# Transposing three of four residual chunks by DMA instead of TensorE at the stage borders of a two-layer hybrid trunk

## The chip, the cores and the metric

The kernel runs on one core of a Trainium2 chip, as one program. The metric is the device time of one execution in microseconds (us). The core's engines run side by side, each through its own list of instructions in order: PE (TensorE, matmuls and transposes), ACT (ScalarE), DVE (VectorE), POOL (GpSimd) and SP (SyncE, which here does nothing but issue DMAs). They wait for one another by semaphores.

## What is computed

Two layers over 256 tokens of width 2048. Cut to what matters here:

```
for l in range(DEPTH):                                  # 2
    hn = rms_norm(h, norm_w[l])
    proj = hn @ w_in[l]                                 # stage "in"
    y = concatenate([deltanet(proj), hgrn2(proj)])      # the two groups of heads
    h = h + y @ w_out[l]                                # stage "out"
    gate = sigmoid(h @ w_ple_gate[l])                   # stage "gate"
    h = h + (p[l] @ w_ple_up[l]) * gate                 # "up", inside the stage "gate"
return rms_norm(h, final_norm_w)
```

All is float32. The residual `h` lies with tokens on the partitions, in four tiles `h[c]` of 128 x 2 x 512 (token, half of the tokens `m`, column), one for each chunk `c` of 512 columns. A matmul needs its left operand with the contracted columns on the partitions, so each time the residual is the input of a stage it has to be transposed. This occurs at three **borders**: out to gate in layer 0 (names `g0`), gate to in of layer 1 (`n1`) and out to gate in layer 1 (`g1`).

## The kernel before

**Products.** Each weight tile is read from memory once, by a DMA of SP into one of three buffers `raw` (L415). ACT rounds it into `whi` (L434) and DVE takes the rest `wlo = raw - whi` (L436), three buffers each; the activations are taken apart in the same way into `hi` and `lo` by `split` (L507). `products` (L448) then issues three matmuls for one product: hi by hi, lo by hi, hi by lo, all at L373. A **step** is one weight tile of 128 x 1024: two slices of 128 rows, two halves of the tokens, three products, 12 matmuls of 128x512. In a step that neither starts nor ends an accumulation the eight matmuls with `whi` come first, and the four with `wlo` last.

**Order.** `run_step` (L469) writes a step's matmuls in program order, after `ahead` (L439) has asked for the preparation of weights two steps on and for loads up to four steps on, as far as the buffers go. PE's list stays in the order written; a scheduler places the instructions of ACT, DVE and SP between one another. All other work is written as generators, which `tick` (L395) moves on by one at each step: `yield 4` means four steps later. The numbers in `DELAY` and `DELAY_AT` say how many.

**Stages.** In the stages out and gate, chunks 0 and 1 of the columns alternate, then chunk 2 runs, then chunk 3. When chunk `c` of out is summed, `after_out` (L1196) adds it into `h[c]` on DVE, waits a few steps, and calls `turn`; `after_gate` (L1202) does the same behind the gate's exp and ln on ACT.

**The transposition.** `turn` (L526) moves one chunk: two banks of PSUM, each filled by four PE transposes of 128x128 (L531), and `split` reads them on ACT and DVE. So a turn costs PE eight instructions, ACT two or four, DVE as many.

**Other names.** Tag `et` has two buffers of 128 x 1024, used in the stage in by `evict` (L619). `tmp` has six of 128 x 512.

Of the kernel before, what the change touches and what calls it, by code (L numbers as in the profile page):

```python
# [8 lines left out]
F32 = mybir.dt.float32  # L9
F32R = mybir.dt.float32r  # L10
I32 = mybir.dt.int32
AF = mybir.ActivationFunctionType
ALU = mybir.AluOpType
PSUM = bass.MemoryType.PSUM
# [18 lines left out]
def chunk_cols(chunk):  # L33

    return [(START[k], 16) if k == "ba" else (START[k] + 256 * g, 256) for k, g in chunk]
# [25 lines left out]
}  # L61


def delay(kind, g, step):
    return DELAY_AT.get(f"{kind}{g}{step}", DELAY[kind][step])
# [106 lines left out]
def trunk(ctx: ExitStack, tc: tile.TileContext, head, xT, x, pT, W, par, fw, cst, msk, eye, out):  # L172
    nc = tc.nc
# [12 lines left out]
    V, S, G = nc.vector, nc.scalar, nc.gpsimd  # L186
# [3 lines left out]
    h = [hp.tile([128, 2, 512], F32, name=f"h{c}") for c in range(4)]  # L190
    pr = cp.tile([128, NPAR], F32, name="pr")
    cs = cp.tile([128, 544], F32, name="cs")
    ms = cp.tile([128, NMASK], I32, name="ms")

# [9 lines left out]
    def xk(k, n=1):  # L204
        o = (0 if k // 4 else NNW) + T * (k % 4)
        return xt[k // 4][:, o:o + T * n]
# [58 lines left out]
    def first_prep():  # L265
# [5 lines left out]
        for k, cs_ in ((0, (0, 1)), (1, (0, 1)), (2, (0,)), (3, (0,)), (2, (1,)), (3, (1,))):  # L271
            if 0 in cs_:
                kp, sl, x, sc = k // 2, slice(T * (k % 2), T * (k % 2) + T), xk(k), xt[0][:, k:k + 1]
                S.activation(a[kp][0][:, sl], x, AF.Copy, scale=sc)
            for c in cs_:
                n, wsl = unit(c, k)
                if k or c:
                    S.activation(w[n][0][:, wsl], raw[n][:, wsl], AF.Copy)
                else:
# [53 lines left out]
    def P(name, i, n=1):  # L333
        o = PAR[name][0] + i
        return pr[:, o:o + n]
# [11 lines left out]
    def gate_constants():  # L347

        S.activation(negA, P("alog", 0, DEPTH * 16), AF.Exp)
        V.tensor_scalar(negA, negA, -1.0, None, ALU.mult)  # L350
# [4 lines left out]
        for l in range(DEPTH):  # L355
            V.tensor_tensor(ee[:, l], lg[l], mx, ALU.subtract)
        S.activation(ee, ee, AF.Exp)
        den = sp.tile([128, 8], F32, tag="lb2", name="den")
# [62 lines left out]
    def prep(n):  # L421
# [11 lines left out]
        for sl in parts:  # L433
            S.activation(hi[:, sl], raw[:, sl], AF.Copy)  # L434
        for sl in parts:
# [48 lines left out]
    def tmp(name, shape=(128, 512)):  # L484
        return tp.tile([128, 512], F32, tag="tmp", name=name)

    def sigmoid(dst, src, e=None):

        if e is None:
            S.activation(dst, src, AF.Exp, scale=-1.0)  # L490
            V.tensor_scalar(dst, dst, BIG, 1.0, ALU.min, ALU.add)
# [15 lines left out]
    def split(src, kp, scales, name):  # L507

        hi = ap_.tile([128, 2 * T], F32R, tag="ahi", name=f"{name}hi{kp}")
        lo = ap_.tile([128, 2 * T], F32R, tag="alo", name=f"{name}lo{kp}")  # L510
        if scales is None:
            S.activation(hi, src, AF.Copy)
            V.tensor_tensor(lo, src, hi.bitcast(F32), ALU.subtract)
            return hi, lo
        w = 2 * T // len(scales)
        for j, sc in enumerate(scales):
            S.activation(hi[:, w * j:w * j + w], src[:, w * j:w * j + w], AF.Copy, scale=sc)
        for j, sc in enumerate(scales):
            sl = slice(w * j, w * j + w)
            V.scalar_tensor_tensor(lo[:, sl], src[:, sl], sc, hi[:, sl].bitcast(F32), ALU.mult, ALU.subtract)  # L520
        return hi, lo

    def norm_scales(l, kp):
        return [P("nw", l * KT + 2 * kp + j) for j in range(2)]

    def turn(c, name, scales):  # L526

        out = []
        for half in range(2):
            ps = pm.tile([128, 512], F32, tag="m", name=f"{name}t{c}{half}")  # L530
            for j in range(2):  # L531
                for m in range(2):
                    k = 2 * half + j
                    PE.transpose(ps[:, 256 * j + 128 * m:256 * j + 128 * m + 128], h[c][:, m, 128 * k:128 * k + 128], ident)
            out.append(split(ps, 2 * c + half, scales(2 * c + half), name))
        return out

    first_ss = []
# [51 lines left out]
    def mix(tag, n, bufs, name):  # L590
        return mp.tile([128, n], F32, tag=tag, name=name, bufs=bufs)
# [604 lines left out]
    def after_out(c, ps, hact, l):  # L1196
        for m in range(2):
            V.tensor_tensor(h[c][:, m], ps[m], h[c][:, m], ALU.add)
        yield delay("b", c, "o")
        hact[2 * c:2 * c + 2] = turn(c, f"g{l}", lambda kp: None)  # L1200

    def after_gate(c, ps, up, act, st, l):  # L1202
        t = [tmp(f"pg{l}{c}{m}") for m in range(2)]
        if l + 1 == DEPTH:
            for m in range(2):
                S.activation(t[m], ps[m], AF.Tanh, scale=0.5)
        else:
            for m in range(2):
                S.activation(t[m], ps[m], AF.Exp, scale=-1.0)
            for m in range(2):  # L1210
                V.tensor_scalar(t[m], t[m], BIG, 1.0, ALU.min, ALU.add)
            for m in range(2):
                S.activation(t[m], t[m], AF.Ln)
                S.activation(t[m], t[m], AF.Exp, scale=-1.0)
        for m in range(2):
            if l + 1 == DEPTH:
                V.scalar_tensor_tensor(t[m], t[m], 1.0, up[m], ALU.add, ALU.mult)
            else:
                V.tensor_tensor(t[m], up[m], t[m], ALU.mult)
            V.tensor_tensor(h[c][:, m], h[c][:, m], t[m], ALU.add)  # L1220
            st.add(c, m)
            if l + 1 == DEPTH:
                G.tensor_tensor(h[c][:, m], h[c][:, m], fwt[c // 2][:, 512 * (c % 2):512 * (c % 2) + 512], ALU.mult)
        if l + 1 < DEPTH:
            yield delay("b", c, "g")
            act[2 * c:2 * c + 2] = turn(c, f"n{l + 1}", lambda kp: norm_scales(l + 1, kp))

    class Finish:

# [66 lines left out]
    act = [None] * (KT // 2)  # L1296
    first_loads()
    for l in range(DEPTH):
# [25 lines left out]
        for c, k4 in order:  # L1324
# [5 lines left out]
            w = 2 if sum(n for _, n in chunk_cols(ch)) > 272 else 4  # L1330
# [30 lines left out]
        hact = [None] * (KT // 2)  # L1361
        chunks, order = stage_plan("out", l)
        ps = {}
        for c, k4 in order:
            if c not in ps:
                ps[c] = banks(f"out{l}{c}", c)
            for q in (0, 2):
                while not pairs_ready(y, k4[q:q + 2]):
                    tick()
                run_step(ps[c], y)  # L1370
            if k4[3] == OUT_KTS[-1]:
                spawn(after_out(c, ps[c], hact, l))
            if c == 2 and k4[0] == OUT_KTS[0]:
                pin = tmp(f"pin{l}")
                nc.scalar.dma_start(out=pin.rearrange("p (j t) -> p j t", j=2), in_=pT[l])
                pact = [split(pin, 0, [0.5] if l + 1 == DEPTH else None, f"p{l}")]
# [6 lines left out]
        act = [None] * (KT // 2)  # L1383
        chunks, order = stage_plan("gate", l)
        ps = {}
        for c, k4 in order:
            if c not in ps:
                ps[c] = banks(f"gate{l}{c}", c)
                if l + 1 == DEPTH and c == 3:

                    ps[c][1] = [ps[c][1], pm.tile([128, 512], F32, tag="m", name="gaterun")]
            for q in (0, 2):
                end = l + 1 == DEPTH and c == 3
                if k4[q + 1] == KT - (9 if end else 1):
                    up = [pm.tile([128, 512], F32, tag="m", name=f"up{l}{c}{m}") for m in range(2)]
                    run_step(up, pact)
                if end and k4[q + 1] == KT - 9:
                    break
                while not pairs_ready(hact, k4[q:q + 2]):
                    tick()  # L1400
                run_step(ps[c], hact)
            if end and k4[3] == KT - 9:

                n = state["next"]
                for i in range(5):
                    ahead(n + i)
                    products(n + i, 0, ps[c], hact)
                half0 = Finish(0, ps[c], up, st)
                for r in range(2):
                    for i in range(5):  # L1410
                        products(n + i, 1, ps[c], hact, run=r)
                last_norm(half0, Finish(1, ps[c], up, st))
                break
            if k4[3] == KT - 1:
                spawn(after_gate(c, ps[c], up, act, st, l))
# [35 lines left out]
```

## Time and profile before

| what | value |
|---|---|
| median of 3 runs | 1242.79 us (1240.89 to 1245.74) |
| the profiled execution: its own time | 1241.43 us |
| its span, first to last instruction | 1239.7 us |
| DVE busy over the span | 882.2 us (71%) |
| ACT busy over the span | 771.9 us (62%) |
| POOL busy over the span | 75.3 us (6%) |
| memory traffic, mean | 176 GB/s |
| border g0: out ends, gate starts | 516.85 us |
| border g1: out ends, gate starts | about 1131.6 us |

A profile lists each instruction with engine, line, tile names (`out<-in`, the buffer numbers left out) and shape. The share of busy time is a mean over stages with different limits; the **chain of work that ended last** tells what set the end, and the **waits** tell for whom an engine stood still. PE's matmuls overlap: a matmul of 128x512 lasts 0.39 us by its record, but a step of twelve takes 2.72 us, 0.227 us each. Idle time of an engine that isn't the bottleneck costs nothing.

### The profile page before, as it was taken

The numbers are of one execution on the slowest core, as the hardware profiler recorded it, in microseconds if no ns is written. First come the engines' busy times: TensorE is split into PE (matmuls) and PEld (weight loads), VectorE is DVE, ScalarE is ACT, GpSimd is POOL, SyncE is SP. The second block draws the span as 40 slices with busy tenths as digits, with TensorE's granted clock in tenths as the row PEclk, the third lists the DMA queues.
The fourth block names the chain that finished last, engine by engine and source line by source line (L and its number), as shares of the span: only waits on it lengthen the run. The fifth ranks groups of instructions, "written<-read, shape, count | busy, mean of one in ns | idle before, by whom it ended". The sixth has DMA issues, their size and how long they took to land.

```text
span 1239.7 us, 21567 instructions
## 1 busy us (share of the span) xinstructions
PE 1226.5 (99%) x8354; PEld 1030.9 (83%) x8354; DVE 882.2 (71%) x1537; ACT 771.9 (62%) x1340; POOL 75.3 (6%) x67
## 2 busy tenths in 40 slices
PE   9999999999999999999999999999999999999997
PEld 8888888888888888888888888878888888888886
DVE  7777897887568656547668878886875696555565
ACT  7676766686757644437666667674867676444453
POOL 0310000000000100000003100000000010000021
PEclk9999999999999999999999999999999999999999
DMA  8455455535354445555555555555444555655563
GB/s 289 175 193 178 158 176 179 175 136 186 140 216 153 171 178 187 180 194 188 178 183 178 178 174 175 171 178 160 133 151 142 183 155 175 207 182 179 183 204 136
DMA packets 74006, 218.69 MB, mean 176 GB/s; under 512 B 15536, under 2 KB 21040, under 8 KB 73904
## 3 DMA queue, kind: packets, MB, share of 16 engines
q1 hardware_dynamic: 63680, 211.93, 51.2%
q10 hardware_dynamic: 10224, 5.39, 1.6%
q8 instruction: 65, 1.06, 0.3%
q14 instruction: 37, 0.30, 0.1%
HBM read 212.84 MB, written 4.46 MB: 175 GB/s over the span
## 4 chain that ended last, share of the span: by engine, by line
PE 89%; DVE 5%; ACT 2%; DMA 2%; issue 1%; SPq 0%; POOLq 0%; POOL 0%; ACTq 0%; DVEq 0%
PE out L373 14%; PE gate L373 13%; PE in1dk L373 7%; PE in0dv L373 6%; PE in1dv L373 6%; PE in0hi L373 6%; PE in1hf L373 5%; PE in0dk L373 5%; PE in0hf L373 5%; PE in1hi L373 5%; DVE wlo L436 2%; PE up L373 2%; DMA raw<-W 2%; PE in0dz L373 1%; PE in1dz L373 1%
## 5 line engine op out<-in xcount | busy, mean ns | idle before, releaser
L436 DVE TENSOR_TENSOR wlo<-raw,whi 128x1024 fp32r<-128x1024 f32 (+2 forms) x393 | 479.9, 1224 | 285.1 <-ACT whi L434 280.2
L434 ACT ACTIVATE whi<-raw 128x1024 fp32r<-128x1024 f32 (+2 forms) x393 | 409.8, 1045 | 309.6 <-PE out L373 89.1
L373 PE MATMUL in1hf<-whi,n1hi 128*128 128x512 f32 x128 | 41.3, 404 | 0.0
L373 PE MATMUL in1hi<-whi,n1hi 128*128 128x512 f32 x128 | 41.0, 402 | 0.0
L373 PE MATMUL in1dk<-whi,n1hi 128*128 128x512 f32 x128 | 40.4, 397 | 0.0
L373 PE MATMUL in1hf<-whi,n1lo 128*128 128x512 f32 x128 | 40.0, 394 | 0.0
L373 PE MATMUL in1hi<-whi,n1lo 128*128 128x512 f32 x128 | 39.7, 391 | 0.0
L373 PE MATMUL gate<-whi,g0hi 128*128 128x512 f32 x128 | 39.7, 391 | 0.0
L373 PE MATMUL in1dk<-whi,n1lo 128*128 128x512 f32 x128 | 39.6, 390 | 0.0
L373 PE MATMUL gate<-whi,g0lo 128*128 128x512 f32 x128 | 39.5, 390 | 0.0
L373 PE MATMUL in1dv<-whi,n1hi 128*128 128x512 f32 (+1 forms) x128 | 36.5, 376 | 0.0
L373 PE MATMUL gate<-whi,g1hi 128*128 128x512 f32 (+1 forms) x120 | 35.7, 379 | 0.0
L373 PE MATMUL gate<-whi,g1lo 128*128 128x512 f32 (+1 forms) x120 | 35.7, 379 | 0.0
L373 PE MATMUL in1dk<-wlo,n1hi 128*128 128x512 f32 x128 | 35.6, 390 | 0.0
L373 PE MATMUL in1hf<-wlo,n1hi 128*128 128x512 f32 x128 | 35.6, 390 | 0.0
L373 PE MATMUL in1hi<-wlo,n1hi 128*128 128x512 f32 x128 | 35.6, 390 | 0.0
L373 PE MATMUL gate<-wlo,g0hi 128*128 128x512 f32 x128 | 35.6, 390 | 0.0
L373 PE MATMUL in1dv<-whi,n1lo 128*128 128x512 f32 (+1 forms) x128 | 34.9, 364 | 0.0
L373 PE MATMUL gate<-wlo,g1hi 128*128 128x512 f32 (+1 forms) x120 | 32.6, 380 | 0.0
L373 PE MATMUL in1dv<-wlo,n1hi 128*128 128x512 f32 (+1 forms) x128 | 31.5, 363 | 0.0
L373 PE MATMUL in0hi<-whi,n0hi 128*128 128x512 f32 x96 | 30.8, 402 | 0.0
L373 PE MATMUL in0hf<-whi,n0hi 128*128 128x512 f32 x96 | 30.7, 401 | 0.0
(1485 smaller groups left out, 2895.3 us busy)
## 6 DMA issues: line engine op xcount, KB each, us to landing
raw<-W SPq DMA_DIRECT2D x383, 512.0 KB, 3.6
raw<-W SPq DMA_DIRECT2D x7, 544.0 KB, 3.7
h<-x SPq DMA_DIRECT2D x4, 512.0 KB, 4.8
xt<-xT SPq DMA_DIRECT2D x3, 512.0 KB, 6.2
out_dram<-h SPq DMA_DIRECT2D x5, 256.0 KB, 2.3
di0d<-di0Bt ACTq DMA_DIRECT2D x4, 256.0 KB, 2.3
di1d<-di1Bt ACTq DMA_DIRECT2D x4, 256.0 KB, 2.3
fw<-fw ACTq DMA_DIRECT2D x2, 512.0 KB, 6.3
```

What stands on the lines that cost most here:

```text
L373: return tc.keep_in_program_order(nc.tensor.matmul(*a, **k))
L434: S.activation(hi[:, sl], raw[:, sl], AF.Copy)
L436: V.tensor_tensor(lo[:, sl], raw[:, sl], hi[:, sl].bitcast(F32), ALU.subtract)
```

## The change

For chunks 0, 1 and 2 a new `turn_by_dma` takes the place of `turn`, at all three borders; chunk 3 keeps `turn`. The DMA moves elements of 16 bits, so each float is cut into its two halves:

1. ACT copies `h[c][:, m]`, seen as 16-bit integers, into the tile `flat` (names `g0p`, `n1p`, `g1p`) with all low halves in one block and all high halves in another. One copy of 1024 elements for each `m`.
2. SP issues one transposing DMA of 128 x 2048 halves (512 KB), in 16 blocks of 128x128, into `across` (`g0q`, `n1q`, `g1q`).
3. ACT joins low and high halves again into float tiles (`g0t`, `n1t`, `g1t`), one copy of 1024 elements for each half chunk.
4. `split` goes on as before, but from these tiles and no longer from PSUM.

Both `flat` and `across` are of tag `et`, which has two buffers: one chunk takes both. `XB` holds the ticks between these parts.

```
+U16 = mybir.dt.uint16
...
+XB = 1, 1, 4, 1, 1
...
+    def turn_by_dma(c, name, scales):
+
+        u16 = lambda ap: ap.bitcast(U16)
+        flat, across = (u16(mix("et", 1024, 2, f"{name}{x}{c}")).rearrange("p (w k m b) -> p w k m b", w=2, k=4, m=2)
+                        for x in "pq")
+        for m in range(2):
+            S.copy(flat[:, :, :, m], u16(h[c][:, m]).rearrange("p (k b w) -> p w k b", k=4, w=2))
+            yield XB[m]
+        every = lambda ap: ap.rearrange("p w k m b -> p (w k m) b")
+        nc.sync.dma_start_transpose(every(across), flat.rearrange("p w k m b -> p (w k m b)"))
+        yield XB[2]
+        out = []
+        for half in range(2):
+            t = tmp(f"{name}t{c}{half}")
+            S.copy(u16(t).rearrange("p (b w) -> p w b", w=2),
+                   across[:, :, 2 * half:2 * half + 2].rearrange("p w k m b -> p w (k m b)"))
+            yield XB[3 + half]
+            out.append(split(t, 2 * c + half, scales(2 * c + half), name))
+        return out
...
     def after_out(c, ps, hact, l):
         for m in range(2):
             V.tensor_tensor(h[c][:, m], ps[m], h[c][:, m], ALU.add)
-        yield delay("b", c, "o")
-        hact[2 * c:2 * c + 2] = turn(c, f"g{l}", lambda kp: None)
+        if c < 3:
+            hact[2 * c:2 * c + 2] = yield from turn_by_dma(c, f"g{l}", lambda kp: None)
+        else:
+            yield delay("b", c, "o")
+            hact[2 * c:2 * c + 2] = turn(c, f"g{l}", lambda kp: None)
...
-            yield delay("b", c, "g")
-            act[2 * c:2 * c + 2] = turn(c, f"n{l + 1}", lambda kp: norm_scales(l + 1, kp))
+            scales = lambda kp: norm_scales(l + 1, kp)
+            if c < 3:
+                act[2 * c:2 * c + 2] = yield from turn_by_dma(c, f"n{l + 1}", scales)
+            else:
+                yield delay("b", c, "g")
+                act[2 * c:2 * c + 2] = turn(c, f"n{l + 1}", scales)
```

How it moves instructions is shown at border g0. PE's list loses 72 transposes (nine turns of eight) and is otherwise the same. First ACT's list around chunk 0; before the change (`h_85` is chunk 0 of the residual, `h_86` chunk 1; numbers of `whi` and `raw` differ between the two programs, the rows stand for the same weights):

```order
L434 ACTIVATE whi_5153<-raw_5115 128x1024 [waits DMAHW7_49,DVE_49,PE_49]
L434 ACTIVATE whi_5173<-raw_5133 128x1024 [waits DMAHW0_49,DVE_49,PE_49]
L434 ACTIVATE whi_5191<-raw_5151 128x1024 [waits DMAHW1_49,DVE_49,PE_49]
L434 ACTIVATE whi_5213<-raw_5171 128x1024 [waits DMAHW2_49,DVE_49,PE_49]
L434 ACTIVATE whi_5249<-raw_5189 128x1024 [waits DMAHW3_49,DVE_49,PE_49]
```

And with the change:

```order
L548 COPY g0p_5171<-h_85 128x8x128 [waits DVE_49]
L438 ACTIVATE whi_5176<-raw_5133 128x1024 [waits DMAHW0_49,PE_49,Activation_49]
L548 COPY g0p_5171<-h_85 128x8x128 [waits DVE_49]
L438 ACTIVATE whi_5195<-raw_5151 128x1024 [waits DMAHW1_49,PE_49,Activation_49]
L438 ACTIVATE whi_5221<-raw_5174 128x1024 [waits DMAHW2_49,PE_49,Activation_49]
L548 COPY g0p_5214<-h_86 128x8x128 [waits DMAHW3_49,DVE_49,Activation_49]
L548 COPY g0p_5214<-h_86 128x8x128 [waits DVE_49]
L438 ACTIVATE whi_5240<-raw_5193 128x1024 [waits DMAHW4_49,PE_49]
```

Four copies of 1024 halves have come between the roundings of weights. The first copy of chunk 1 (`g0p_5214`) waits for a DMA: its buffer is the one that the transposing DMA of chunk 0 reads.

Next on ACT, the joins. Before the change, from the rounding that follows `whi_5249`'s step, with the splits out of PSUM (`g0t`):

```order
L512 ACTIVATE g0hi_5234<-g0t_5229 128x512 [waits PE_49]
L512 ACTIVATE g0hi_5243<-g0t_5238 128x512 [waits PE_49]
L434 ACTIVATE whi_5291<-raw_5211 128x1024 [waits DMAHW4_49,DVE_49,PE_49]
L512 ACTIVATE g0hi_5270<-g0t_5265 128x512 [waits PE_49]
L512 ACTIVATE g0hi_5279<-g0t_5274 128x512 [waits PE_49]
L512 ACTIVATE p0hi_5285<-pin_5283 128x512
L434 ACTIVATE whi_5309<-raw_5247 128x1024 [waits DMAHW5_49,DVE_49,PE_49]
```

And with the change, from the row after `whi_5240`:

```order
L556 COPY g0t_5299<-g0q_5172 128x2x512
L556 COPY g0t_5323<-g0q_5172 128x2x512
L438 ACTIVATE whi_5265<-raw_5219 128x1024 [waits DMAHW5_49,PE_49,Activation_49]
L516 ACTIVATE g0hi_5319<-g0t_5299 128x512 [waits Activation_49]
L516 ACTIVATE g0hi_5343<-g0t_5323 128x512 [waits Activation_49]
L438 ACTIVATE whi_5283<-raw_5238 128x1024 [waits DMAHW6_49,DVE_49,PE_49]
L556 COPY g0t_5347<-g0q_5215 128x2x512 [waits DMAHW0_49]
L438 ACTIVATE whi_5303<-raw_5263 128x1024 [waits DMAHW7_49,DVE_49,PE_49]
L516 ACTIVATE g0hi_5367<-g0t_5347 128x512 [waits Activation_49]
```

The joins `g0t` stand ahead of roundings of weights, and the join of chunk 1 (`g0t_5347`) waits for the second transposing DMA while `whi_5303` is queued behind it. The rounding of the input embedding (`p0hi`) has gone to an earlier place.

Last, SP's list at the same place, with the change (before it, the same rows of `raw` follow one another with nothing between):

```order
L419 DMA raw_5174<-W 128x1024 [waits DMAHW7_49,DVE_49]
L551 DMA_TRANSPOSE g0q_5172<-g0p_5171 128x16x128 [waits DMAHW3_49,PE_49,Activation_49]
L419 DMA raw_5193<-W 128x1024 [waits DMAHW0_49,DVE_49]
L419 DMA raw_5219<-W 128x1024 [waits DMAHW1_49,DVE_49]
L419 DMA raw_5238<-W 128x1024 [waits DMAHW2_49,DVE_49]
L419 DMA raw_5263<-W 128x1024 [waits DMAHW4_49,DVE_49]
L551 DMA_TRANSPOSE g0q_5215<-g0p_5214 128x16x128 [waits DMAHW3_49,Activation_49]
L419 DMA raw_5281<-W 128x1024 [waits DMAHW5_49,DVE_49]
```

Each transposing DMA stands in SP's list between loads of weights and waits for ACT: the first for the copies into `g0p_5171`, the second for the joins that empty `g0q_5172`, whose buffer it fills. The loads behind it wait with it.

## The prediction

> **What bounds the kernel now.** I read the page first: busy time, the granted clock in 40 slices, and the chain of work that ended last.
>
> ```profile
> span 1239.7 us, 21567 instructions
> PE 1226.5 (99%) x8354; PEld 1030.9 (83%) x8354; DVE 882.2 (71%) x1537; ACT 771.9 (62%) x1340; POOL 75.3 (6%) x67
> PEclk9999999999999999999999999999999999999999
> PE 89%; DVE 5%; ACT 2%; DMA 2%; issue 1%; SPq 0%; POOLq 0%; POOL 0%; ACTq 0%; DVEq 0%
> ```
>
> PE is busy all the time at full clock, and the chain is PE for 89%. The waits of PE say whether it ever stands still near the borders:
>
> ```profile
> PE hg10yp L376 <- DVE hg10yt L601: 1.3, 1, 1.3
> PE hg11pa L373 <- issue: 1.2, 1, 1.2
> PE warm L373 <- DVE zeros L249: 1.1, 1, 1.1
> ```
>
> None of its longest waits is at a border. There the chain is PE alone. So a PE instruction taken out of a border shortens the run by its whole pitch, as long as no new wait comes in its place.
>
> **What the change removes.** The chain, asked in windows at the three borders, has each turn as a piece of its own (start, length, what). These are the nine turns that go:
>
> ```profile
> 473.44 0.88 PE g0t L376 x8
> 477.08 0.87 PE g0t L376 x8
> 497.05 0.87 PE g0t L376 x8
> ...
> 572.34 0.87 PE n1t L376 x8
> 586.87 0.88 PE n1t L376 x8
> 606.84 0.87 PE n1t L376 x8
> ...
> 1088.07 0.87 PE g1t L376 x8
> 1091.71 0.88 PE g1t L376 x8
> 1111.68 0.87 PE g1t L376 x8
> ```
>
> One transpose is recorded with 0.273 us, but eight overlap to 0.87 us on the chain. Nine turns are 9 x 0.875 = **7.9 us**. That is all the change can win.
>
> **What it adds on ACT.** Four copies of 1024 elements for each chunk. No row has a 16-bit copy. The nearest by element count is the rounding of a weight tile:
>
> ```profile
> L434 ACT ACTIVATE whi<-raw 128x1024 fp32r<-128x1024 f32 x379 | 400.5, 1058 | 305.3 <-PE out L373 89.1 <-PE gate L373 62.5 <-PE in1dk L373 19.1
> 478.53 0.64 ACT L512 ACTIVATE p0hi<-pin 128x512 fp32r<-128x512 f32 x1
> ```
>
> Bounds: 0.64 us if it goes by bytes like 512 floats, 2.1 us if 16-bit halves at a stride cost double; I take 1.06 us. 36 copies are 38 us of ACT time, where ACT idles 305 us before `whi` alone, nearly all waiting for PE to free a buffer. The splits cost the same from SBUF (`p0hi`, 0.64 us) as from PSUM. DVE gets no instruction more.
>
> **What it adds on SP and the DMA queues.** Nine transposing DMAs. Call T the time from SP's issue to landing; the trace has none. The neighbours:
>
> ```profile
> raw<-W SPq DMA_DIRECT2D x383, 512.0 KB, 3.6
> di0Tt<-d SPq DMA_DIRECT2D x8, 16.0 KB, 3.9
> ...
> q1 hardware_dynamic: 63680, 211.93, 51.2%
> q10 hardware_dynamic: 10224, 5.39, 1.6%
> ...
> L415 SPq DMA_DIRECT2D raw<-W x9: 327/328/328, 455.4 to 478.5; - x9
> DMA to landing us min/median/max: 3.4/3.5/3.6
> ...
> L688 SPq DMA_DIRECT2D di0Tt<-d x8: 333/434/1162, 193.3 to 201.6; - x8
> ```
>
> A weight load of the same 512 KB on the same queue lands in 3.5 us. By q1 its data take 0.512 x 1239.7 x 0.524/211.93 = 1.6 us of all engines, so 1.9 us are fixed. The queue with small packets, q10, takes 0.016 x 1239.7 / 10224 = 1.94 ns per packet. If the transposition moves in rows of one block, 128 halves or 256 B, it has 2048 packets, 4.0 us, T = 5.9. If it moves in the smallest pieces this kernel has, 64 B in `di0Tt<-d` (16 floats), it has 8192, T = 17.8. So T lies between 3.5 and 17.8 us. I take 3.5 to 5.9, nearest to the row with the same size, queue and partitions; the sum below is the same over that span. The Trainium skill, "Advanced Engine Details and Errata", section X-Bar Transpose (TRN2), says transposing DMAs are as fast as regular ones, 350 to 400 GB/s; by it T is an estimated 3.3 us and the sum is the same. No run here shows one yet.
>
> **Does that hide?** The dangerous place is border g0 (g1 is alike), chunks 0 and 1. First the rows of before:
>
> ```profile
> 463.94 0.69 DVE L1198 TENSOR_TENSOR h<-out,h 128x512 f32<-128x512 f32 x1
> 465.31 0.69 DVE L1198 TENSOR_TENSOR h<-out,h 128x512 f32<-128x512 f32 x1 [0.67 <-PE out L373]
> ...
> 464.85 1.06 ACT L434 ACTIVATE whi<-raw 128x1024 fp32r<-128x1024 f32 x1 [2.11 <-PE out L373]
> 470.29 1.06 ACT L434 ACTIVATE whi<-raw 128x1024 fp32r<-128x1024 f32 x1 [2.11 <-PE out L373]
> 482.57 1.06 ACT L434 ACTIVATE whi<-raw 128x1024 fp32r<-128x1024 f32 x1 [1.67 <-PE out L373]
> ...
> 486.00 0.62 PE L373 MATMUL out<-whi,dn02hi 128*128 128x512 f32 x2
> ```
>
> A `whi` is rounded as soon as PE frees its buffer and is used two whole steps later: the one of 482.57 is used by the step after 486.00, at 488.72, so it may start 5 us late before PE feels it. That is the cover. Now ACT's list with the change, in order. The first copy starts when `h[0]` is added, 464.63, and ends 465.69; `whi_5176` to 466.75; second copy to 467.81, and SP issues the first DMA. `whi_5195` and `whi_5221` end at 471.35. The two copies of chunk 1 wait for that DMA: 467.81 + T. Then two copies, `whi_5240` and two joins, 5 x 1.06: the second DMA goes out at 473.11 + T and lands at 473.11 + 2T; ACT's work in between (2 x 1.06 + 2 x 0.64) is shorter. Then the join and `whi_5303`, 2.12: done at 475.23 + 2T. PE wants it at 488.72 less two turns, 486.96. So PE waits when **T exceeds 5.9 us**, and then 2 us for each us of T, as both DMAs stand in this row. At T = 3.5 there are 4.7 us to spare. If SP itself is held for all of T, the load behind the first DMA lands at 471.3 + T, 1.4 us later than ACT wants it, and the limit is 5.2.
>
> Chunk 2 and border n1 have more room:
>
> ```profile
> 494.36 0.69 DVE L1198 TENSOR_TENSOR h<-out,h 128x512 f32<-128x512 f32 x1 [0.67 <-PE out L373]
> 502.54 1.06 ACT L434 ACTIVATE whi<-raw 128x1024 fp32r<-128x1024 f32 x1 [1.19 <-PE out L373]
> ...
> 555.00:575.00 20.00, 20.00 (x94) 16.64 (x93) 15.82 (x21) 17.81 (x31) 0.00 (x0) 1.00 0.52 186
> 563.76 1.07 ACT L434 ACTIVATE whi<-raw 128x1024 fp32r<-128x1024 f32 x1
> 595.78 0.61 PE L373 MATMUL gate<-whi,g0hi 128*128 128x512 f32 x2
> ```
>
> Chunk 2: issue 2.5 us after the second add starts, 496.86; landing, two joins and the `whi` of 502.54 end at 500.04 + T; wanted 6.15 us after 502.54 less one turn, 507.81: T up to 7.7. At n1 ACT is 17.81 of 20 us busy, so I add its list up from 563.76: six copies, six `whi`, and 6.6 us of exp, ln, squares and splits put the second DMA at 583.1; T, two joins, two splits and a `whi`, 4.0 us, against 595.78 less two turns, 594.0: T up to 6.9.
>
> So the stall is 4(T - 5.9) + 2(T - 7.7) + (T - 6.9), each bracket from zero up. With T from 3.5 to 5.9 it is nothing, and the **sum is -7.9 us**: 1241.43 of the profiled execution becomes 1233.5, and from the median 1242.79, 0.1% above it, **1234.9 us**. About 0.5%, 6.2 us, is what a measurement can tell from no change. I call the result faster below 1236.6 (T up to 6.3), and slower above 1249 (T from 8.6).
>
> **Rivals.**
>
> *The blocks go one after another.* The DMA has 16 blocks. Eight DMAs in a row from SP, `di0Tt<-d`, take 0.434 us of SP each and land 3.9 us on: 16 x 0.434 + 3.9 = 10.8 us. Stall 19.6 + 6.2 + 3.9 = 29.7, net +21.8: **1265 us**, slower. Loads of weights wait behind on SP too. For it: a shape of 128x16x128 that no DMA here has. Against: a load of 128 rows takes SP only 0.33 us. It decides from T = 7.7, where the stall eats the gain. The Trainium skill, "VectorE: DVE Perf Modes", section The three transpose paths, has 1309 ns for one 128x128 by DMA and, in its Rules for kernel authors, advises TensorE where PSUM will do; 16 of them in a row would make an estimated T of 20.9 and 1335 us. No row here bears on it yet.
>
> *Small pieces.* With 64 B pieces, T = 17.8: stall at least 47.6 + 20.2 + 10.9 = 78.7, **1314 us**, and the weight loads share the DMA engines, now half busy.
>
> *Dear copies, or T a little over the limit.* At 2.1 us a copy, 475.23 + 2T grows by eight copies to 483.7 + 2T, at T = 3.5 a stall of 3.7 for each g border; at n1 some 5. Net about +5, **1248 us**; with T = 7.5 instead, -7.9 + 7.0, 1242. Both count as no change.
>
> *It does not take PE's time off.* PE's order stays, only the transposes go; another wait already behind PE could come out and keep the end: **1243 us**. The chain at the borders is PE alone, so this is small.
>
> **How the numbers follow.** Forecast, hidden (T up to 6.3): 0.50, of which 0.01 falls below the 0.5%. Dear copies or T of 6.3 to 8.6: 0.18. Blocks one after another: 0.20. Small pieces: 0.10. PE's time stays: 0.02. Faster 0.49, same 0.01 + 0.18 + 0.02 = 0.21, slower 0.30. The range starts at 1232, the full gain from the lower runs (1240.89 - 7.9 = 1233) and one more for scatter; it reaches to 1267, past the block-by-block case, and leaves out the small pieces and the worse half of blocks.
>
> **What would show it.** Right: no `g0t`, `n1t`, `g1t` transposes on PE for three chunks; PE's waits have no new row at the borders; time to landing of the transposing DMA under 6 us; ACT's copies near 1.06 us. Wrong: a row `PE out` or `PE gate` that waits for ACT `whi` or DVE `wlo`; ACT waiting several us at the join or at the copy of chunk 1 for the DMA; SP long in the transposing instruction with `whi` then waiting for `raw`.

## The result and the profile after

| kernel | median us | lowest to highest | runs | ratio to before |
|---|---|---|---|---|
| before | 1242.82 | 1240.89 to 1245.74 | 7 | |
| with the change | 1235.11 | 1232.26 to 1238.49 | 7 | 0.994 [0.9922, 0.9958] |

The change takes 7.7 us off, 0.6%; by the interval of the ratio it is 5.2 to 9.7 us. Forecast were 1234.9 us. The profiled execution took 1233.27 us, 8.2 less than that of before.

The page of the changed kernel, in the order in which the prediction read that of before (busy times, clock, queue 1, the chain's shares; then the loads of weights):

```profile
span 1231.6 us, 21477 instructions
PE 1216.1 (99%) x8282; PEld 1021.8 (83%) x8282; DVE 880.9 (72%) x1537; ACT 807.7 (66%) x1376; POOL 75.3 (6%) x67
PEclk9999999999999999999999999999999999999999
...
q1 hardware_dynamic: 82400, 216.65, 54.7%
...
PE 93%; ACT 4%; issue 1%; DMA 1%; DVE 1%; POOLq 0%; POOL 0%; ACTq 0%; DVEq 0%
...
raw<-W SPq DMA_DIRECT2D x383, 512.0 KB, 3.6
```

PE has 72 instructions fewer and is still busy for 99%, at full clock: it bounds the kernel as before, with less to do. ACT has 36 instructions and 35.8 us more (807.7 - 771.9). Weight loads land 3.6 us after their issue, as before.

Did something else become late? The waits of PE in the changed kernel, all of them (in total us, times, longest us):

```profile
PE hg11pa L377 <- issue: 2.2, 1, 2.2
PE hg00yp L380 <- DVE hg00yt L625: 1.3, 1, 1.3
PE hg10yp L380 <- DVE hg10yt L625: 1.3, 1, 1.3
PE warm L377 <- DVE zeros L253: 1.1, 1, 1.1
PE dn00pg L377 <- DVE dn00kq L855: 0.6, 1, 0.6
PE gate L377 <- ACT pg L1236: 0.2, 1, 0.2
```

One row is new at a border, and it is small: `gate` waits 0.2 us for ACT's exp `pg`. It comes back below. The row `hg11pa` has grown from 1.2 to 2.2 us; it stands in the stage in of layer 1, away from the borders, and differs between executions of one kernel (2.6 in the repeat e7). The chain of the changed kernel at border g0 (start, length, what) shows that the turns of chunks 0 to 2 are gone and nothing has taken their place; what is left is chunk 3's, behind the first step of gate:

```profile
457.23 57.15 PE out L377 x252
514.38 2.73 PE gate L377 x12
517.11 0.87 PE g0t L380 x8
```

**Stage lengths.** The gain is as large as the scatter of single runs, so I also read where it falls. PE's list stays in order, so the time from the first matmul of a stage to the first of the next is that stage's length. The marks on PE's timeline (start, time, what), before:

```profile
421.82 0.71 PE L373 MATMUL out<-whi,hg00hi 128*128 128x512 f32 x2
...
516.85 0.62 PE L373 MATMUL gate<-whi,g0hi 128*128 128x512 f32 x2
...
618.47 0.41 PE L373 MATMUL in1dz<-whi,n1hi 128*128 128x272 f32 x2
...
1036.48 0.71 PE L373 MATMUL out<-whi,hg10hi 128*128 128x512 f32 x2
...
1131.48 0.62 PE L373 MATMUL gate<-whi,g1hi 128*128 128x512 f32 x2
```

And with the change:

```profile
421.99 0.48 PE L377 MATMUL out<-whi,hg00hi 128*128 128x512 f32 x1
...
514.22 0.62 PE L377 MATMUL gate<-whi,g0hi 128*128 128x512 f32 x2
...
613.63 0.41 PE L377 MATMUL in1dz<-whi,n1hi 128*128 128x272 f32 x2
...
1031.09 0.71 PE L377 MATMUL out<-whi,hg10hi 128*128 128x512 f32 x2
...
1123.31 0.62 PE L377 MATMUL gate<-whi,g1hi 128*128 128x512 f32 x2
```

The same three differences for every kernel of this study, each from its one profiled execution:

| kernel | run, us | out 0 (g0, chunks 0-2) | gate 0 (g0, chunk 3; n1, chunks 0-2) | out 1 (g1, chunks 0-2) |
|---|---|---|---|---|
| before | 1242.8 | 95.03 | 101.62 | 95.00 |
| the change | 1235.1 | 92.23 | 99.41 | 92.22 |
| the change again (e7) | 1235.2 | 92.24 | 99.51 | 92.23 |
| only g0 and g1 by DMA (e1) | 1238.3 | 92.32 | 101.52 | 92.23 |
| only n1 by DMA (e2) | 1241.6 | 94.93 | 99.57 | 95.00 |
| all four chunks by DMA (e3) | 1233.0 | 92.22 | 98.78 | 92.45 |
| all four again (e8) | 1233.3 | 92.23 | 98.97 | 92.53 |
| PE's transposes back, unread (e4) | 1244.2 | 94.95 | 102.96 | 94.93 |
| each transposing DMA twice (e5) | 1254.1 | 95.65 | 109.20 | 95.28 |
| each copy twice (e6) | 1257.4 | 95.64 | 111.60 | 96.76 |
| e5, exp ahead of the joins (e9) | 1247.9 | 96.32 | 104.12 | 95.35 |
| all four, exp ahead of the joins (e10) | 1233.9 | 92.23 | 97.92 | 92.46 |

Three turns less shorten the stage out by 2.80 and 2.78 us, and gate 0 by 2.21: together 7.79 of the 8.1 us between the spans. Parts that the change doesn't touch differ more between executions: in the stage in of layer 1 the stretch from the first `in1dz` to the first `in1dv` took 239.8 us with the change and 241.2 in its repeat. PE's granted clock goes with that. Around the wait at `hg11pa` it fell to 0.50: for 6.8 us, from 845 us on, in e1 and e2, where the stretch took 242.6 and 241.7 us; for 3.4 us in before (from 847 us on, 240.4 us) and in the repeat (from 844 us on); not at all in the change's own execution. (The slices of the page are 31 us long and don't show it.) In the three stages of the table the clock stood at 1.00 throughout, except in e5, e6 and e9. So the lengths of these stages tell tenths of a us here, and run times whole ones.

**The new work.** The instructions of the transposing line in the changed kernel (ns of SP's time min/median/max, first and last start), the time to landing over all nine, and the groups of copies by form (busy us, mean ns):

```profile
L551 SPq DMA_TRANSPOSE g0q<-g0p x3: 1427/1757/3087, 467.8 to 495.9; - x3
L551 SPq DMA_TRANSPOSE n1q<-n1p x3: 3419/3471/3855, 564.7 to 599.2; - x3
L551 SPq DMA_TRANSPOSE g1q<-g1p x3: 1669/1744/3067, 1076.9 to 1105.2; - x3
...
DMA to landing us min/median/max: 4.3/5.2/5.9
```

```profile
L556 ACT COPY g0t<-g0q 128x1024 uint16<-128x1024 uint16 x6 | 7.8, 1346 | 3.9 <-DMA g0q<-g0p 3.9
...
L548 ACT COPY g0p<-h 128x1024 uint16<-128x1024 uint16 x6 | 6.1, 1040 | 4.8 <-DVE h L1222 3.8 <-DMA g0q<-g0p 0.9
```

T was 4.3 to 5.9 us, inside the 3.5 to 5.9 that were taken. The copies apart cost 1.04 us, the joins 1.35. SP is held 1.4 to 3.9 us by each transposing DMA, against 0.33 by a weight load. Queue 1 has 18720 packets more, 2080 for each of the nine DMAs: 2048 rows of 256 B and 32 packets of 4 B. By the trace's packet records a row took 24 ns on one engine, so that each DMA took 3.0 us of the sixteen engines' time; the 512 KB of a weight load, in packets of 4096 B, took 1.6 us. The share of queue 1 can't give this price: it is 54.7% here and 56.1% in the repeat of the same kernel.

### The profile page after: what moved, and what is told of

It is laid out like the page before. It is cut to its first block, busy times and chain, and to the rows that moved or that the text cites. A ratio compares the mean times of both kernels' runs of the same rounds, so it can differ in the third digit from the quotient of the medians.

```text
span 1231.6 us, 21477 instructions
## 1 busy us (share of the span) xinstructions
PE 1216.1 (99%) x8282; PEld 1021.8 (83%) x8282; DVE 880.9 (72%) x1537; ACT 807.7 (66%) x1376; POOL 75.3 (6%) x67
## 3 DMA queue, kind: packets, MB, share of 16 engines
q1 hardware_dynamic: 82400, 216.65, 54.7%
q8 instruction: 65, 1.06, 0.3%
## 4 chain that ended last, share of the span: by engine, by line
PE 93%; ACT 4%; issue 1%; DMA 1%; DVE 1%; POOLq 0%; POOL 0%; ACTq 0%; DVEq 0%
PE out L377 14%; PE gate L377 11%; PE in0hf L377 7%; PE in1hf L377 7%; PE in1dk L377 7%; PE in1hi L377 7%; PE in0hi L377 7%; PE in0dv L377 6%; PE in1dv L377 6%; PE in0dk L377 5%; PE up L377 1%; ACT whi L438 1%; PE in0dz L377 1%; PE in1dz L377 1%; DMA n1q<-n1p 0%
```

## The experiments

**One part alone.** Does each border bring its own three turns? In e1 border n1 goes back to TensorE, in e2 g0 and g1 do.

```
# e1, in after_gate                # e2, in after_out
-            if c < 3:             -        if c < 3:
+            if c < 0:             +        if c < 0:
```

> Only the six turns at the borders g0 and g1 go by DMA; the three at n1 are back on TensorE. Theory (the run gains the chain pitch of each transpose that leaves PE, 0.875 us a turn, and nothing else shows): 6 x 0.875 = 5.25 us below before, about 1237.6 us, and no wait of PE at g0 or g1. Rival (the gain comes from one border, or from banks of PSUM and ACT time set free): the step isn't proportional to the turns; if n1 carries it, this run lies within 2 us of before, if n1 costs something (PE's new wait of 0.25 us there), it lies at or below 1235.1.

> Only the three turns at n1 go by DMA; g0 and g1 are back on TensorE. Theory: 3 x 0.875 = 2.6 us less the 0.25 us that PE waits there in the trace of after, so 2.4 us below before, about 1240.4 us, and with the g-only run the two gains add up to that of the whole change, 7.7 us. Rival (n1, where ACT and DMA take the chain for 29 us, costs PE more than one profile shows): no gain or a loss against before.

Measured: e1 1238.25 us (1237.88 to 1239.85), ratio 0.9967 [0.9955, 0.9979]; e2 1241.59 us (1239.99 to 1244.53), 0.9999 [0.9987, 1.001]. For e1 the forecast holds. For e2 it doesn't: its interval leaves a gain of 1.6 us at most, where 2.4 were expected, and the gains of the two medians, 4.3 and 1.0 us, don't add up to 7.7. The trace of e2 does show n1's gain: gate 0 is 2.05 us shorter and both stages out are as before. But the stretch from `in1dz` to `in1dv` took 241.7 us against 240.4 before, 1.3 more, where the only edit that reaches in is the turn of chunk 3, the same in both; there the clock was 0.50 for 6.8 us instead of 3.4. The mean granted clock of e2's eleven runs is 0.9954, and 0.9974 in the runs of before beside them, so most of them may have lost time in this way. Whether the DMAs at n1 bring it about isn't shown: the change and its repeat have the same ones, and the clock there fell for 0 and 3.4 us.

**All four chunks.** The fourth turn of each border goes too.

```
-        if c < 3:
+        if c < 4:
...
-            if c < 3:
+            if c < 4:
```

> Chunk 3 goes by DMA too, at all three borders: three more turns leave PE. Its result is needed only in the last quarter of the next stage's first two chunks, some 12 steps of 2.72 us = 33 us after its sum; a turn by DMA took about 14 us of steps from the first copy to the last split. Theory: another 3 x 0.875 = 2.6 us, about 1232.5 us, 10.3 us below before. Rival (chunk 3 stands where the next stage begins; its copies and its DMA stand before the roundings of weights and, at n1, before the norm factors): PE waits at the start of the next stage, 2 us or more a border, and the run is at 1238 or above.

Measured: 1233.03 us (1231.63 to 1237.0), ratio 0.9924 [0.9909, 0.9938], 2.1 us below the change: near the 2.8 that three more turns are worth. PE still doesn't wait at g0 and g1.

The change and this version were run once more, beside each other:

> The change itself once more, beside the others on the same chip: 1235.1 us, 7.7 below before, and the same stages in its trace: 92.2 us from the first out matmul to the first gate matmul in both layers.

> The version with all four chunks by DMA once more, beside the change on the same chip. Theory: three more turns of 0.875 to 0.93 us are gone, less some 0.3 us of PE's wait at n1: 2.3 us below the change, about 1232.8 us. Rival (the first pair of runs was scatter): no difference from the change.

Measured: 1235.15 us (1233.26 to 1235.57), 0.9936 [0.992, 0.9953], and 1233.29 us (1232.81 to 1236.77), 0.993 [0.9912, 0.9948]. The medians are 1.9 us apart, and the first two were 2.1. The intervals overlap, so that all four chunks are better than three rests on both pairs together, and on gate 0, shorter by 0.63 and 0.54 us.

**PE's work put back.** If PE's pitch is all the gain, and ACT, SP and the DMA are hidden, then PE doing its 72 transposes beside the new way must come out at the time of before. They write banks that nobody reads.

```
         nc.sync.dma_start_transpose(every(across), flat.rearrange("p w k m b -> p (w k m b)"))
+        for half in range(2):
+            ps = pm.tile([128, 512], F32, tag="m", name=f"{name}dead{c}{half}")
+            for j in range(2):
+                for m in range(2):
+                    k = 2 * half + j
+                    PE.transpose(ps[:, 256 * j + 128 * m:256 * j + 128 * m + 128], h[c][:, m, 128 * k:128 * k + 128], ident)
         yield XB[2]
```

> The change as it is, but PE also does the 72 transposes of chunks 0 to 2 into banks that nobody reads, so PE's list is as long as before while ACT, SP and DMA carry the new path. Theory (all of the gain is PE's pitch; ACT's 36 copies, the nine DMAs and the splits from SBUF are hidden and worth nothing either way): back at before, 1242.8 us, within 1.5 us. Rival (part of the gain is from splits that no longer wait for PE, or from banks that come free): clearly below before, by 3 us or more. Rival (the new path costs something that the gain covers): above before by as much.

Measured: 1244.17 us (1242.7 to 1248.44), ratio 1.0016 [1.0005, 1.0026], so 0.6 to 3.2 us above before. The stages out are back at 94.95 and 94.93, within 0.1 us of before: at g0 and g1 all that the change adds is hidden. Gate 0 is 1.34 us longer than before, of which the waits of PE in this kernel explain most:

```profile
PE n1dead L380 <- DVE h L1253: 1.0, 1, 1.0
```

The added transposes stand sooner behind the sum than the old turn did and wait for `h`. That is this experiment's own doing.

**The DMA twice.** The same transposing DMA is issued a second time behind the first, so that T and SP's hold grow. Here the limits of the prediction can be tried.

```
         nc.sync.dma_start_transpose(every(across), flat.rearrange("p w k m b -> p (w k m b)"))
+        nc.sync.dma_start_transpose(every(across), flat.rearrange("p w k m b -> p (w k m b)"))
```

> Each transposing DMA of the change is issued twice, the second waiting until the first has landed, so T from first issue to last landing is about twice the 4.3 to 5.9 us that the trace of after shows: 9 to 11 us. ACT's and SP's lists are placed anew: several roundings of weights now stand ahead of the copies and joins that wait for the DMA. Theory A (the prediction's sum holds as it stands, 4(T - 5.9) + 2(T - 7.7) + (T - 6.9)): at T = 9.5 a stall of 20.6 us, about 1256 us. Theory B (the limit isn't T but what is queued behind the waiting copy; with the roundings ahead of it the cover is longer, and only loads behind the second DMA on SP come late): 0 to 3 us above the change, 1235 to 1238 us. Rival (the added DMA traffic slows every weight load): raw takes well over 3.6 us to land, and PE waits for whi that waits for raw.

Measured: 1254.12 us (1251.32 to 1255.24), ratio 1.0093 [1.0074, 1.0111]. The cover ends, and the total is near the 1256 us of theory A. But the places are other ones: against the change, the stages out lose 3.4 and 3.1 us, where the formula at T = 9.5 had 9.0 for each, and gate 0 loses 9.8, where it had 2.6. T was longer besides: from the first issue of a pair to the second landing the nine pairs took 9.6 to 11.0 us, 10.3 in the middle, and there the formula gives a stall of 26 us, where 19.0 were measured. That the totals meet is chance. Theory B (0 to 3 us) falls as well, and so does the rival of slower weight loads, which still landed in 3.6 us. The waits of PE in this kernel name the largest loss:

```profile
PE gate L377 <- ACT pg L1237: 6.7, 1, 6.7
...
PE out L377 <- ACT whi L438: 2.1, 4, 1.0
...
PE gate L377 <- DVE h L1223: 1.3, 2, 0.7
PE out L377 <- DVE h L1223: 1.1, 1, 1.1
```

`pg` is the exp of the gate. It reads the sums of chunk 2 out of PSUM, and PE can't start chunk 3 before it has freed their banks. On ACT's timeline of this kernel (in brackets: idle time before, and what ended it) the exp stands behind the joins of chunk 1, which wait for the DMA:

```profile
594.18 1.06 ACT L438 ACTIVATE whi<-raw 128x1024 fp32r<-128x1024 f32 x1 [3.32 <-DMA raw<-W]
597.43 2.51 ACT L557 COPY n1t<-n1q 128x1024 uint16<-128x1024 uint16 x2 [2.20 <-DMA n1q<-n1p]
599.82 1.69 ACT L521 ACTIVATE n1hi<-n1t,pr 128x256 fp32r<-128x256 f32 x4
601.42 1.06 ACT L1237 ACTIVATE pg<-gate 128x512 f32<-128x512 f32 x2
```

And on PE's timeline the first matmul of chunk 3 starts when the first of these two exps is done:

```profile
602.04 1.22 PE L377 MATMUL gate<-whi,g0hi 128*128 128x512 f32 x2 [6.66 <-ACT pg L1237]
...
604.77 1.05 PE L377 MATMUL gate<-whi,g0hi 128*128 128x512 f32 x2
```

The wait costs more than its own length. From 600.4 to 607.2 us the granted clock is 0.50, and until then a pair of matmuls starts every 0.85 us instead of every 0.45. Half of the 5.15 us from 602.04 on is some 2.6 us more; with the wait that is 9.3 of the 9.8 us.

**The copies twice.** The two copies apart and the two joins are each done twice.

```
             S.copy(flat[:, :, :, m], u16(h[c][:, m]).rearrange("p (k b w) -> p w k b", k=4, w=2))
+            S.copy(flat[:, :, :, m], u16(h[c][:, m]).rearrange("p (k b w) -> p w k b", k=4, w=2))
...
             S.copy(u16(t).rearrange("p (b w) -> p w b", w=2),
                    across[:, :, 2 * half:2 * half + 2].rearrange("p w k m b -> p w (k m b)"))
+            S.copy(u16(t).rearrange("p (b w) -> p w b", w=2),
+                   across[:, :, 2 * half:2 * half + 2].rearrange("p w k m b -> p w (k m b)"))
```

> Each of the 36 ACT copies (1.04 us into the 16-bit tile, 1.35 us out of it) is done twice: 43 us more on ACT, the same data. Theory: at g0 and g1, where ACT has idle time before nearly every rounding, it is hidden (under 1 us each); at n1, where ACT is busy without a break for some 30 us, the 9.6 us of chunks 0 and 1 don't fit, and PE waits there 4 to 8 us: about 1241 us. Rival (the order of the list, not ACT's load, is the limit, as the prediction reckoned with a fixed order): PE waits some 6 us at each g border too, and the run is at 1253 or above. Rival (ACT has room at n1 too): 1235 to 1237.

Measured: 1257.37 us (1255.19 to 1260.0), ratio 1.0119 [1.0099, 1.0139]. The theory fell: doubled copies aren't hidden anywhere. The stages out lose 3.4 and 4.5 us, gate 0 12.2. The waits of PE in this kernel:

```profile
PE gate L377 <- ACT pg L1239: 6.0, 1, 6.0
PE out L377 <- ACT whi L438: 5.3, 2, 2.7
```

The exp is the largest again, and behind it the clock is 0.50 here too, from 602.4 to 609.3 us. At the stages out it is the rounding of weights, as the prediction's walk had it; with 2.7 us each these waits are shorter than the 6 of the rival. So ACT's cover is between one and two times what the change uses.

**The exp ahead of the joins.** Two experiments now point at the exp; neither has moved it. In e9 and e10 the joins of chunk 1 at n1 come three ticks later, so that they stand behind the exps of chunk 2 in ACT's list. e9 is e5 with this, e10 is the version with all four chunks with it.

```
-        yield XB[2]
+        yield 7 if name[0] == 'n' and c == 1 else XB[2]
```

> The run with each DMA issued twice, and one number more changed: at n1, chunk 1 waits 7 ticks instead of 4 between its DMA and its joins, so ACT's exp of the sums of chunk 2 (pg from gate) stands ahead of those joins. In the doubled run PE stood 6.7 us in one piece at n1 for that exp, whose banks of PSUM it needs for the next chunk's sums. Theory (PE waits for banks that the exp frees, because the exp is queued behind joins that wait for the DMA): that wait is gone, the stage from the first gate matmul to the first of the next in falls from 109.2 to about 103, and the run from 1254 to about 1248 us. Rival (what is late is the roundings of weights or the loads behind the DMA, and the exp is only seen last): PE waits as long for whi or wlo instead, and the run stays at 1252 or above.

> All four chunks by DMA, with the same 7 ticks for chunk 1 at n1 (DMAs issued once). Theory: PE's wait of 0.5 us at n1 for the exp is gone, the stage from first gate to first in matmul falls from 98.97 to 98.5 us, the run ends 0.5 us below the version without it, about 1232.5 us, which the run times alone can't tell. Rival: the wait moves to another operand and the stage keeps its length.

Measured: e9 1247.85 us (1246.66 to 1249.1), ratio 1.0042 [1.0028, 1.0057], 6.3 us below e5 by the medians and 3.1 by the profiled executions; gate 0 goes from 109.20 to 104.12. The waits of PE in e9, between 510 and 650 us:

```profile
PE in1dz L377 <- ACT whi L438: 1.6, 1, 1.6
PE gate L377 <- ACT whi L438: 1.4, 1, 1.4
PE gate L377 <- DVE h L1223: 0.9, 1, 0.9
PE gate L377 <- ACT pg L1237: 0.3, 1, 0.3
```

The wait for `pg` falls from 6.7 to 0.3 us by an edit of the joins' place alone: the exp's place was the cause of it. The clock stays at 1.00 in gate 0. Not all is won: in this window PE now waits 3.0 us for `whi`, where e5 had no such wait, so behind the exp the roundings of weights are next to be late, as the rival had it in part.

e10: 1233.86 us (1230.88 to 1235.1), 0.9928 [0.9913, 0.9942]. Gate 0 is 97.92, 1.05 below e8 where 0.5 was expected, and PE has no wait between 510 and 650 us. That is the full worth of its four turns: 101.62 - 97.92 = 3.70, four times 0.93. In the run time e10 can't be told from e8. The fastest kernels of this study are these versions with all four chunks, 1233 to 1234 us, 9 us below before.

## Why the prediction was right, and where not

**PE bounds, and a turn taken out is worth its pitch: right, the pitch a little low.** The chain gave 0.875 us for a turn. Measured are 2.80 / 3 = 0.93, since the matmuls behind a turn come late as well: in the trace of before, the first two pairs behind a turn start 0.55 us apart (474.06 and 474.61), others 0.45. e1, e3 and e4 show the same figure from both sides: out stages of 92.2 to 92.5 without three turns, 94.9 to 95.0 with them.

**T: right, with one part too dear.** The value taken came from the 1.9 us of a weight load that don't go by its size and from 2048 packets of 256 B at 1.94 ns. The packets are these, but they took 1.5 ns each, 3.0 us instead of 4.0. The landings of 4.3 to 5.9 us fill the range taken up to its end. The two rivals that rested on other shapes of the transfer fall: blocks one after another (T = 10.8) and pieces of 64 B (8192 packets). The Trainium skill, "VectorE: DVE Perf Modes", section The three transpose paths, has 1309 ns for one 128x128 by DMA; the estimate of 20.9 us for 16 of them in a row doesn't hold here, where all 16 blocks landed in 5.9 us at most, and the TensorE that its rules advise was the engine short of time. The Trainium skill, "Advanced Engine Details and Errata", section X-Bar Transpose (TRN2), calls such a DMA as fast as a regular one. This holds nearly for the landing, 4.3 to 5.9 us against 3.6 for a weight load of the same size, but not for the engines' time, 3.0 us against 1.6.

**The copies on ACT: right for the ones apart, low for the joins.** 1.04 and 1.35 us against 1.06. Both move 1024 elements of 16 bits; the first read the halves at a stride of two, the second write them so.

**The walk at g0: right.** It had the first DMA go out at 467.81 us and the second at 473.11 + T, which is 477.7 with the 4.6 us that the first one took; they went out at 467.79 and 477.93. It had PE want `whi_5303` at 486.96 us. In the changed kernel the step that uses it starts at 487.01, and the rounding ended at 485.07: 1.9 us to spare. ACT's timeline of the changed kernel shows the two waits that the walk named, each short:

```profile
472.49 1.99 ACT L548 COPY g0p<-h 128x1024 uint16<-128x1024 uint16 x2 [0.94 <-DMA g0q<-g0p]
...
482.80 1.35 ACT L556 COPY g0t<-g0q 128x1024 uint16<-128x1024 uint16 x1 [1.99 <-DMA g0q<-g0p]
484.02 1.05 ACT L438 ACTIVATE whi<-raw 128x1024 fp32r<-128x1024 f32 x1
```

**SP: one sign was there and did no harm.** SP was held for 1.4 to 3.9 us, less than all of T, and ACT waited 3.3 us in two pieces for `raw` around g0; none of it reached PE.

**The step that was wrong: n1, "T up to 6.9".** It added up ACT's list as far as a `whi`, and asked when PE wants that `whi`. The first thing late at n1 is something else in the same list, the exp that frees the banks. The chain of the changed kernel leaves PE just there:

```profile
578.81 5.92 DMA n1q<-n1p
584.75 2.04 ACT n1t L556 x2
...
590.35 18.00 PE gate L377 x78
```

and PE's timeline has the wait at its end:

```profile
589.49 0.61 PE L377 MATMUL gate<-wlo,g0hi 128*128 128x512 f32 x2
590.35 0.73 PE L377 MATMUL gate<-whi,g0hi 128*128 128x512 f32 x2 [0.25 <-ACT pg L1236]
```

The pair of 589.49 leaves PE to the next one 0.45 us later, at 589.94, so PE started 0.4 us late (the 0.25 in brackets counts from the end of the pair's record). The limit at n1 is then about 5.92 - 0.4 = 5.5 us, not 6.9, and it was already passed. The `whi` that the walk asked about was not late. In the times of the changed kernel, whose gate starts 2.6 us sooner, the walk wants it at 591.4; the rounding behind the joins and splits ended at 589.03. The exp costs little here: gate 0 won 2.21 us where three turns are worth 2.80, some 0.6 us. That the exp is the cause is shown by e9 and e10, in kernels where its wait was longer. That the sum came out so closely is luck in part: two small errors go against each other, as three times three turns of 0.93 are 8.4 us instead of 7.9 and n1 gave 0.6 of it back, and the interval is wider than both.

**The formula for the stall: wrong beyond its limits.** With T above 5.9 it has 4 us for each us at both g borders together, some 18 at the 10.3 us of e5. e5 lost 6.5 there, about a third. The formula kept ACT's list as the change has it, two roundings behind the first copies and then the copies of chunk 1, which wait for the DMA. In e5 ACT's timeline has four roundings there, the last two of them ahead of that wait:

```profile
474.91 1.06 ACT L438 ACTIVATE whi<-raw 128x1024 fp32r<-128x1024 f32 x1 [2.48 <-DMA raw<-W]
476.34 1.06 ACT L438 ACTIVATE whi<-raw 128x1024 fp32r<-128x1024 f32 x1 [0.37 <-PE out L377]
479.74 1.99 ACT L548 COPY g0p<-h 128x1024 uint16<-128x1024 uint16 x2 [2.34 <-DMA g0q<-g0p]
```

The scheduler places them anew for each kernel, and so less stands behind the wait; that this is the whole of the difference isn't shown. How the 3 to 4.5 us that e5 and e6 lose at g0 and at g1 divide stays open.

**The rival of dear copies** had the right mechanism and a price between the ends: 1.35 us for two of the four cost no more than part of the 0.6 us at n1. At 2.1 us for each it was given +5 us against before; e6, with 2.1 us for each half apart and 2.7 for each join, came to +15.2 (1257.4 against 1242.2 for before in the same session), 10.0 of it in gate 0.

## What to carry to other kernels

On an engine that is busy all the time, an instruction taken off was worth its pitch and a little more; when that is near the scatter of runs, read the lengths of the stages in the trace, and the granted clock beside them. When work goes to another engine, walk through everything in that engine's list behind the new wait, the instructions that free banks and buffers as well as those that feed operands: here the exp was late before any weight was. Where ACT and SP have room, float tiles can be transposed as 16-bit halves by DMA, and the place of the joins in ACT's list decides what it costs.

## What the runs showed of the hardware

- A transposing DMA of 128 x 2048 halves holds SP for 1.4 to 3.9 us (a weight load of the same bytes 0.33), in the change longest at n1. Two, one behind the other, held the loads of weights behind them: in e5 around g0, ACT's waits have

```profile
ACT whi L438 <- DMA raw<-W: 12.5, 5, 4.7
```

  while the loads, once issued, landed in 3.6 us as ever. So the delay arises ahead of the issue, in SP's list, and not from the traffic: there SP also stood 3.3 us until the first DMA of a pair had landed.
- The rows of 256 B of a transposing DMA took 24 ns each on a DMA engine, the packets of 4096 B of a weight load 198 ns in the same trace: twice the time for each byte.
- Ways to copy 1024 halves differ on ACT: 1.04 us with strided reads, 1.35 with strided writes.
- In e5 and e6 PE stood still for 6.7 and 6.0 us. About 5 us after it had stopped, the granted clock fell to 0.50 and stayed there for 6.8 us, most of it in the work behind the wait.
